# RMSNorm, memory-bound: all loads and stores on one hardware queue, in a fixed order, with rows of up to 64 KB

## The chip, the cores and the metric

One core of one Trainium2 chip. The metric is the device time of one execution in microseconds (us). The kernel before takes 165.03 us (median of 4 runs, 164.47 to 165.42). Times of one kernel scatter by about 1 us here, so most kernels were timed in five rounds beside the kernel before.

## The reference

```python
batch, seq, dim = 16, 1024, 512            # 16384 rows of 512 float32
rms = np.sqrt(np.mean(x ** 2, axis=-1, keepdims=True) + 1e-5)
return (x / rms * gamma).astype(np.float32)
```

33.55 MB are read and 33.55 MB written. Nothing is reused, so the transfers alone set a floor.

## The kernel before

Eight tiles of 16 rows per partition (4 MB) go through five buffers. Four engines matter here: SyncE, which only issues transfers, ACT (ScalarE), DVE (VectorE) and POOL (GpSimd). SyncE issues the loads on its hardware queue. POOL issues the stores, 2 MB each, on the software queue. (A queue is also called a ring below.) ACT squares and sums each row, and takes the root of 8 sums at a time. DVE takes the reciprocal and multiplies by it and by gamma, in place.

```python
work = ctx.enter_context(tc.tile_pool(name="work", bufs=5))
...                                                    # cut: pools, gamma broadcast over partitions
nc.gpsimd.dma_start(out=gamma_row, in_=gamma.unsqueeze(0))
...
for t in range(ntiles):                                # 8 tiles
    xt = work.tile([P, G, R, D], fp32)                 # G=2, R=8, D=512
    nc.sync.dma_start(out=xt, in_=xt_view[t].rearrange("p (g r) d -> p g r d", g=G))
    ...
    for g in range(G):
        for r in range(R):
            nc.scalar.activation(out=sq_scratch, in_=xt[:, g, r, :], func=AF.Square,
                                 accum_out=ss[:, g, r : r + 1])
        nc.scalar.activation(out=rms[:, g], in_=ss[:, g], func=AF.Sqrt, bias=eps_t, scale=1.0 / D)
        nc.vector.reciprocal(out=rstd[:, g], in_=rms[:, g])
        for r in range(R):
            nc.vector.scalar_tensor_tensor(out=xt[:, g, r, :], in0=xt[:, g, r, :],
                scalar=rstd[:, g, r : r + 1], in1=gamma_b, op0=OP.mult, op1=OP.mult)
        nc.gpsimd.dma_start(out=ot_view[t][:, g], in_=xt[:, g])
```

## Time and profile before

| | before |
|---|---|
| time, median | 165.03 us |
| span of the profiled run | 163.2 us |
| DVE, ACT busy | 90.4 us, 98.5 us |
| DMA, mean over the span | 411 GB/s |

The first view is the page's table of 40 slices of the span, with its list of DMA queues. A digit is the busy share of the 16 DMA engines in a slice, in tenths; a queue's line gives packets, MB and share of the engines' time.

```profile
span 163.2 us, 536 instructions
...
DMA  7999899999999999999999999999999999999980
GB/s 241 402 442 458 385 474 426 317 440 426 466 414 415 426 446 458 418 409 474 383 418 454 462 426 393 478 389 413 422 434 430 426 442 430 426 434 434 430 369 28
...
q1 hardware_dynamic: 1152, 33.55, 48.6%
q0 software_dynamic: 2336, 33.56, 48.2%
q14 instruction: 3, 0.02, 0.0%
```

The engines are busy in all but the first and the last slices: the kernel is bound by transfers. Two queues share them half and half. The last queue line: three packets of 8 KB on a queue that the program does not use, which the list calls instruction: fetches of instructions. In the packet records they stand at 34.8, 51.8 and 79.4 us, 0.31 us each.

The second view gives busy times in stretches of the span; the last two columns are the mean share of the DMA engines and the rate (PEclk, the clock of TensorE, plays no part here). (A packet seems to be booked whole at its start, so shares over 1 occur.)

```profile
core 0: us, PE busy (x) PEld busy (x) DVE busy (x) ACT busy (x) POOL busy (x), PEclk, DMA share, GB/s
40.00:60.00 20.00, 0.00 (x0) 0.00 (x0) 18.11 (x30) 19.21 (x55) 1.59 (x3) 1.00 1.00 430
60.00:80.00 20.00, 0.00 (x0) 0.00 (x0) 18.10 (x30) 16.12 (x48) 1.59 (x3) 1.00 1.00 429
80.00:100.00 20.00, 0.00 (x0) 0.00 (x0) 13.50 (x22) 11.89 (x34) 1.59 (x3) 1.00 1.01 434
...
158.00:160.00 2.00, 0.00 (x0) 0.00 (x0) 0.00 (x0) 0.00 (x0) 0.00 (x0) 1.00 0.39 164
160.00:162.00 2.00, 0.00 (x0) 0.00 (x0) 0.00 (x0) 0.00 (x0) 0.00 (x0) 1.00 0.06 25
```

In the middle the rate is 429 to 434 GB/s, with loads and stores mixed. The stretch 158 to 160 us has a share of only 0.39, but 160 to 162 us still 0.06: a few engines work on after the others have finished. The records of semaphores show this by engine. Each bulk transfer has 16 such records, read here as one for each engine, when its share of the transfer had landed; these are the 16 times of the last store, sorted (us from the span's start; worked out from the trace, not a view of the page):

```
before: 158.87 158.93 158.96 159.04 159.05 159.06 159.13 159.16 159.17 159.18 159.33 159.34 159.36 160.62 161.41 161.73
```

Thirteen engines end within 0.5 us. Three are 1.3 to 2.4 us later than the last of these. The transfer is done when the last is. From here on, "spread" is the distance from the first to the last of these 16 times; the prediction calls it skew.

The waits of SyncE's queue show when loads had to wait for a free buffer (total us, times, longest):

```profile
SPq L59 <- DMA out_dram<-xt: 97.6, 3, 58.0
```

Three of the eight loads waited for stores to land. The engines had stores to move meanwhile, so this cost nothing by itself.

### The profile page before, as it was taken

The numbers are of one execution on the slowest core, as the hardware profiler recorded it, in microseconds if no ns is written. First come the engines' busy times: TensorE is split into PE (matmuls) and PEld (weight loads), VectorE is DVE, ScalarE is ACT, GpSimd is POOL, SyncE is SP. The second block draws the span as 40 slices with busy tenths as digits, with TensorE's granted clock in tenths as the row PEclk, the third lists the DMA queues.
The fourth block names the chain that finished last, engine by engine and source line by source line (L and its number), as shares of the span: only waits on it lengthen the run. The fifth ranks groups of instructions, "written<-read, shape, count | busy, mean of one in ns | idle before, by whom it ended". The sixth has DMA issues, their size and how long they took to land.

```text
span 163.2 us, 536 instructions
## 1 busy us (share of the span) xinstructions
PE 2.0 (1%) x2; PEld 0.5 (0%) x2; DVE 90.4 (55%) x147; ACT 98.5 (60%) x274; POOL 9.3 (6%) x21
## 2 busy tenths in 40 slices
PE   0050000000000000000000000000000000000000
PEld 0010000000000000000000000000000000000000
DVE  0010098988988988988918890058930298600000
ACT  3007999999999999997499601998008992000000
POOL 2000001011011011011010101001010001100000
DMA  7999899999999999999999999999999999999980
GB/s 241 402 442 458 385 474 426 317 440 426 466 414 415 426 446 458 418 409 474 383 418 454 462 426 393 478 389 413 422 434 430 426 442 430 426 434 434 430 369 28
DMA packets 3491, 67.14 MB, mean 411 GB/s; under 512 B 416, under 2 KB 416, under 8 KB 416
## 3 DMA queue, kind: packets, MB, share of 16 engines
q1 hardware_dynamic: 1152, 33.55, 48.6%
q0 software_dynamic: 2336, 33.56, 48.2%
q14 instruction: 3, 0.02, 0.0%
HBM read 33.56 MB, written 33.55 MB: 411 GB/s over the span
## 4 chain that ended last, share of the span: by engine, by line
DMA 47%; ACT 19%; issue 16%; DVE 3%; POOL 1%; POOLq 0%; SPq 0%
DMA out_dram<-xt 27%; DMA xt<-in_x_dram 21%; ACT sq_scratch L67 17%; DVE xt L84 3%; ACT rms L74 1%; ACT L74 1%; POOL out_dram L93 1%; POOLq L119 0%; DVE rstd L81 0%; POOLq L93 0%; SPq L59 0%
## 5 line engine op out<-in xcount | busy, mean ns | idle before, releaser
L67 ACT ACTIVATE sq_scratch<-xt 128x512 f32<-128x512 f32 x128 | 80.4, 628 | 35.8 <-DMA xt<-in_x_dram 32.3
L84 DVE SCALAR_TENSOR_TENSOR xt<-xt,rstd,gamma_b 128x512 f32<-128x512 f32 x128 | 86.2, 747 | 0.6
L81 DVE RECIPROCAL rstd<-rms 128x8 f32<-128x8 f32 x16 | 3.2, 203 | 40.2 <-ACT rms L74 40.2
L67 ACT ACTIVATION_READ_ACCUMULATOR sq_scratch<-xt 128x1 f32 x128 | 23.9, 186 | 0.0
L93 POOL DMA_DIRECT2D out_dram<-xt x16 | 8.5, 532 | 131.7 <-DVE xt L84 131.7
L51 DVE COPY gamma_b<-gamma_psum 128x512 f32<-128x512 f32 x1 | 0.7, 693 | 9.4 <-PE gamma_psum L49 9.4
L74 ACT ACTIVATE rms<-ss,eps_t 128x8 f32<-128x8 f32 x16 | 4.8, 301 | 0.5
L49 PE MATMUL gamma_psum<-gamma_row,ones_col 1*128 1x512 f32 x2 | 2.0, 1122 | 8.3 <-DMA gamma_row<-in_gamma_dram 8.3
L67 ACT ACT_TABLE_LOAD x1 | 1.3, 1283 | 0.7 <-PEq L108 0.7
L74 ACT ACT_TABLE_LOAD x1 | 1.3, 1283 | 0.0
L45 POOL DMA_DIRECT2D gamma_row<-in_gamma_dram x1 | 0.6, 616 | 0.8 <-POOLq L108 0.8
L47 DVE MEMSET ones_col<- 1x128 f32 x1 | 0.2, 165 | 0.8 <-PEq L108 0.8
L49 PEld LDWEIGHTS gamma_psum<-gamma_row,ones_col 1*128 1x128 f32 x2 | 0.5, 306 | 8.2 <-issue 8.2
L108 POOL MEMSET const-float32-0.0<- 128x1 f32 x1 | 0.1, 98 | 0.2 <-issue 0.2
L108 POOL MEMSET const-bfloat16-1.0<- 128x1 bf16 x1 | 0.1, 101 | 0.0
L108 POOL MEMSET const-float32-1.0<- 128x1 f32 x1 | 0.1, 98 | 0.0
L108 POOL MEMSET const-uint8-127<- 128x1 uint8 x1 | 0.1, 98 | 0.0
L54 DVE MEMSET eps_t<- 128x1 f32 x1 | 0.1, 59 | 0.0
## 6 DMA issues: line engine op xcount, KB each, us to landing
xt<-in_x_dram SPq DMA_DIRECT2D x8, 4096.0 KB, 21.4
out_dram<-xt POOLq DMA_DIRECT2D x16, 2048.0 KB, 37.5
gamma_row<-in_gamma_dram POOLq DMA_DIRECT2D x1, 2.0 KB, 6.9
```

The lines of the kernel that those rows point to most:

```text
L45: nc.gpsimd.dma_start(out=gamma_row, in_=gamma.unsqueeze(0))
L47: nc.vector.memset(ones_col, 1.0)
L49: nc.tensor.matmul(gamma_psum, ones_col, gamma_row, start=True, stop=True)
L51: nc.vector.tensor_copy(out=gamma_b, in_=gamma_psum)
L54: nc.vector.memset(eps_t, eps)
L67: nc.scalar.activation(out=sq_scratch, in_=xt[:, g, r, :], func=AF.Square, accum_out=ss[:, g, r : r + 1],)
L74: nc.scalar.activation(out=rms[:, g], in_=ss[:, g], func=AF.Sqrt, bias=eps_t, scale=1.0 / D,)
L81: nc.vector.reciprocal(out=rstd[:, g], in_=rms[:, g])
L84: nc.vector.scalar_tensor_tensor(out=xt[:, g, r, :], in0=xt[:, g, r, :], scalar=rstd[:, g, r : r + 1], in1=gamma_b, op0=OP.mult, op1=OP.mult,)
L93: nc.gpsimd.dma_start(out=ot_view[t][:, g], in_=xt[:, g])
L108: nc = _bacc.Bacc("TRN2", target_bir_lowering=False, num_devices=1)
```

## The change

The intent is to keep the DMA engines busy without a break and in a planned order. Every load and store goes on SyncE's one hardware queue. Three slots of 32 rows per partition (8 MB) hold the data, so 24 MB are loaded ahead. A row of a transfer is 64 KB or 32 KB per partition, where it was 32 KB for loads and 16 KB for stores. Gamma moves to ACT's queue. The instructions of ACT and DVE stay the same in number and size.

```diff
-    work = ctx.enter_context(tc.tile_pool(name="work", bufs=5))
+    slots = [const.tile([P, R, D], fp32, name=f"slot{i}") for i in range(3)]   # R = 32
+    def load(t, slot, r0, r1):
+        nc.sync.dma_start(out=slots[slot][:, r0:r1], in_=xv[t][:, r0:r1])
+    def store(t, slot, r0, r1):
+        nc.sync.dma_start(out=ov[t][:, r0:r1], in_=slots[slot][:, r0:r1])
+    load(0, 0, 0, 16)
+    load(0, 0, 16, 32)
+    load(1, 1, 0, 32)
+    load(2, 2, 0, 32)
...                                          # cut: views of x and out
-    nc.gpsimd.dma_start(out=gamma_row, in_=gamma.unsqueeze(0))
+    nc.scalar.dma_start(out=gamma_row, in_=gamma.unsqueeze(0))
...                                          # cut: compute(), the same instructions on 8 rows at a time
-            nc.gpsimd.dma_start(out=ot_view[t][:, g], in_=xt[:, g])
+    compute(0, 0, 32)
+    store(0, 0, 0, 32)
+    compute(1, 0, 16)
+    store(1, 1, 0, 16)
+    load(3, 0, 0, 16)
+    load(3, 0, 16, 32)
+    compute(1, 16, 32)
+    store(1, 1, 16, 32)
+    compute(2, 0, 32)
+    store(2, 2, 0, 32)
+    compute(0, 0, 16)
+    store(3, 0, 0, 16)
+    compute(0, 16, 32)
+    store(3, 0, 16, 32)
```

More of the change, by code (lines that the diff above doesn't have):

```diff
@@ L27 @@
     N, D = xf.shape
-    assert N % P == 0
-    R = 8
-    G = 2
-    RG = R * G
-    assert N % (P * RG) == 0
-    ntiles = N // (P * RG)
-    xt_view = xf.rearrange("(t p r) d -> t p r d", p=P, r=RG)
-    ot_view = of.rearrange("(t p g r) d -> t p g r d", p=P, g=G, r=R)
+    R = 32
+    G = 8
+    assert N == 4 * P * R
+    xv = xf.rearrange("(t p r) d -> t p r d", p=P, r=R)
+    ov = of.rearrange("(t p r) d -> t p r d", p=P, r=R)
     const = ctx.enter_context(tc.tile_pool(name="const", bufs=1))
-    work = ctx.enter_context(tc.tile_pool(name="work", bufs=5))
     stats = ctx.enter_context(tc.tile_pool(name="stats", bufs=4))
     psum = ctx.enter_context(tc.tile_pool(name="psum", bufs=1, space=bass.MemoryType.PSUM))
+    slots = [const.tile([P, R, D], fp32, name=f"slot{i}") for i in range(3)]
[7 more added lines that the diff above has]
+    load(2, 2, 0, 32)
     gamma_row = const.tile([1, D], fp32)
-    nc.gpsimd.dma_start(out=gamma_row, in_=gamma.unsqueeze(0))
+    nc.scalar.dma_start(out=gamma_row, in_=gamma.unsqueeze(0))
     ones_col = const.tile([1, P], fp32)
@@ L55, with compute @@
     sq_scratch = const.tile([P, D], fp32)
-    for t in range(ntiles):
-        xt = work.tile([P, G, R, D], fp32)
-        nc.sync.dma_start(out=xt, in_=xt_view[t].rearrange("p (g r) d -> p g r d", g=G))
-        ss = stats.tile([P, G, R], fp32)
-        rms = stats.tile([P, G, R], fp32)
-        rstd = stats.tile([P, G, R], fp32)
-        for g in range(G):
-            for r in range(R):
+    def compute(slot, r0, r1):
+        for g in range(r0, r1, G):
+            ss = stats.tile([P, G], fp32, name="ss")
+            rms = stats.tile([P, G], fp32, name="rms")
+            rstd = stats.tile([P, G], fp32, name="rstd")
+            for r in range(G):
                 nc.scalar.activation(
                     out=sq_scratch,
-                    in_=xt[:, g, r, :],
+                    in_=slots[slot][:, g + r, :],
                     func=AF.Square,
-                    accum_out=ss[:, g, r : r + 1],
+                    accum_out=ss[:, r : r + 1],
                 )
-            nc.scalar.activation(
-                out=rms[:, g],
-                in_=ss[:, g],
-                func=AF.Sqrt,
-                bias=eps_t,
-                scale=1.0 / D,
-            )
-            nc.vector.reciprocal(out=rstd[:, g], in_=rms[:, g])
-            for r in range(R):
+            nc.scalar.activation(out=rms, in_=ss, func=AF.Sqrt, bias=eps_t, scale=1.0 / D)
+            nc.vector.reciprocal(out=rstd, in_=rms)
+            for r in range(G):
                 nc.vector.scalar_tensor_tensor(
-                    out=xt[:, g, r, :],
-                    in0=xt[:, g, r, :],
-                    scalar=rstd[:, g, r : r + 1],
+                    out=slots[slot][:, g + r, :],
+                    in0=slots[slot][:, g + r, :],
+                    scalar=rstd[:, r : r + 1],
                     in1=gamma_b,
```

## The prediction

> **What bounds it.** The 16 DMA engines. The slice table of the page shows DMA at 9 tenths or more in all but four of 40; 67.1 MB move in the 163.2 us span. ACT is busy 98.5 us and DVE 90.4 us (page, part 1) and fit under the transfers. The trace's completions give the rate of one direction alone: the 4-MB loads landed at 12.99 and 22.71 us, 9.72 us apart (432 GB/s), and in the tail, where only stores remain, a 2-MB store lands each 4.86 us (432 GB/s). The stretches 40-60, 60-80 and 80-100 us, with loads and stores mixed, ran at 430, 429 and 434 GB/s. The Trainium skill ("DMA: Bandwidth & Descriptors", section "Where 436 GB/s comes from") puts the ceiling at 435.2 GB/s, within 1% of this trace.
>
> **Budget of before.** 67.1 MB at 432 GB/s: 155.3 us. First packet at 1.73 us. Last landing 161.73 us, then 1.5 us to the span's end. That leaves 4.7 us: first packets 0.6 us longer than the usual 1.21; about 0.7 us of slow load packets at 29-31 us, when the first stores start; about 0.35 us from last packet to landing; some 0.6 us more in the mixed part; and 2.4 us of skew: from the load landing at 123 us on, 13 of the 16 engines complete each transfer within 0.6 us, the other three 1.2 to 2.4 us later.
>
> **What the change does.**
> - Stores leave the software queue: 16 POOL issues of 0.53 us go. They were hidden; SyncE issues of 0.4 us are too: nothing.
> - Packets of 64 KB: a 32-KB packet takes 1.213 us, a 16-KB one 0.611, so at most 9 ns per packet to save; 90 fewer per engine would be 0.8 us, but the landing cadence shows none of it.
> - One queue in a fixed order: engines stop alternating between two rings. The mixed losses become two or three changes of direction. The skew may go if it comes from two rings or from the software queue (the same page, "Latency and other measured facts", calls two engines usually slower, and that specific to the software path; this trace has three late ones, cause not shown). The 8-KB instruction fetches (0.31 us, three in the run) stay.
> - No wait runs the queue dry (estimates from 9.7 us per 4 MB, 6.2 us per 8 rows): loads queued to 60 us, store 0 ready at 45; store 0 ends at 79, next store ready at 60; loads of the fourth block issue at about 80.5 (after store 0 landed), needed at 89; later stores ready at 73, 98, 119, 131, needed at 108, 118, 137, 147. Smallest slack 8 us.
>
> **On the critical path.** Only the 4.7 us residue. I expect 1.2 to 3.5 us of it back. The time (165.19) is 1.9 us over the span; I keep that.
>
> **Predicted** 162.5 us, range 160.6 to 164.4; faster by over 2% 0.33, within 2% 0.65, slower 0.02.
>
> **Right or wrong in the profile.** DMA at 9 tenths in all middle slices; last store's 16 completions within 0.8 us (else the skew is not the queue's); the last landing at 157.5 to 159.5 us; 64-KB packets of 2.41 to 2.43 us; SyncE's longest wait about 45 us before store 0.
>
> **What would make it wrong.** 64-KB rows (256 KB between engines' streams) could run at another HBM rate, either way; changes of direction could drain the engines for over 1 us each; the skew could stay.

## The result

163.16 us (median of 4 runs, 162.68 to 163.86) against 165.03 us. The ratio is 0.9887, with a 95% interval of 0.9852 to 0.9921: a real gain of about 1.1%, within 2%. A ratio here is the mean time of one kernel's runs over that of the other's of the same rounds, so not quite the ratio of the medians quoted. Executions over 1.5% slower than the fastest of the same kernel are left out of the means. A second run of five rounds gave 163.32 us and 0.9904.

The same views after. The page's slices and queues:

```profile
span 161.6 us, 509 instructions
...
DMA  7999999989989999699699999999999799699991
GB/s 260 389 430 478 389 470 438 519 375 405 519 373 405 505 276 487 292 519 487 292 440 454 389 454 454 389 478 430 389 503 519 308 487 503 292 462 430 405 470 49
...
q1 hardware_dynamic: 1728, 67.11, 97.3%
q14 instruction: 3, 0.02, 0.0%
```

One queue now carries all data, in 1728 packets where two queues had 3488. The three instruction fetches are still there. Slices at 6 and 7 tenths in the middle are not idle engines: with 64-KB packets booked at their start a slice can miss or gain a whole packet. The rates over longer stretches show that:

```profile
40.00:60.00 20.00, 0.00 (x0) 0.00 (x0) 15.46 (x26) 16.99 (x48) 0.00 (x0) 1.00 1.04 420
60.00:80.00 20.00, 0.00 (x0) 0.00 (x0) 17.48 (x29) 19.18 (x56) 0.00 (x0) 1.00 0.97 419
80.00:100.00 20.00, 0.00 (x0) 0.00 (x0) 16.62 (x27) 11.77 (x34) 0.00 (x0) 1.00 0.97 417
...
158.00:160.00 2.00, 0.00 (x0) 0.00 (x0) 0.00 (x0) 0.00 (x0) 0.00 (x0) 1.00 0.08 33
160.00:162.00 2.00, 0.00 (x0) 0.00 (x0) 0.00 (x0) 0.00 (x0) 0.00 (x0) 1.00 0.00 0
```

The middle has not become faster: 417 to 420 GB/s here against 429 to 434 before, within what the booking of whole packets can shift (one 64-KB packet on each of 16 engines is 1 MB, or 52 GB/s over 20 us). In the tail 160 to 162 us is empty, where it held 0.06. (The last packets are 32 KB in place of 16, so they are booked earlier, and the share of 158 to 160 us can't be compared with before.) The firm reading is by engine, the last store's 16 landings in the profiled run:

```
after: 158.64 158.68 158.78 158.85 158.86 158.91 158.99 159.01 159.09 159.10 159.13 159.18 159.40 159.54 160.26 160.63
```

The median engine ends as before (159.05 against 159.17 us). Two engines are late in place of three, and by less. The waits of SyncE's queue:

```profile
SPq L44 <- DVE slot L79: 81.7, 5, 22.3
...
SPq L44 <- DMA slot<-in_x_dram: 23.6, 2, 19.9
SPq L41 <- DMA out_dram<-slot: 21.7, 1, 21.7
```

SyncE waits for loads and then for DVE before each store (lines 44 are stores, 41 loads), and once 21.7 us for store 0 to land before it may reload slot 0. None of these leaves the queue dry: the fourth block's loads were issued at 82.6 us, and the store ahead of them in the queue landed at 91 to 92 us.

### The profile page after: what moved, and what is told of

The parts are those of the page before. It is cut to its first block, busy times and chain, and to the rows that moved or that the text cites. A ratio compares the mean times of both kernels' runs of the same rounds, so it can differ in the third digit from the quotient of the medians.

```text
span 161.6 us, 509 instructions
## 1 busy us (share of the span) xinstructions
PE 2.0 (1%) x2; PEld 0.5 (0%) x2; DVE 90.4 (56%) x147; ACT 98.5 (61%) x274; POOL 0.2 (0%) x4
## 3 DMA queue, kind: packets, MB, share of 16 engines
q1 hardware_dynamic: 1728, 67.11, 97.3%
## 4 chain that ended last, share of the span: by engine, by line
DMA 43%; ACT 20%; DVE 17%; issue 2%; DVEq 0%
DMA out_dram<-slot 23%; DMA slot<-in_x_dram 19%; ACT sq_scratch L70 18%; DVE slot L79 16%; ACT rms L76 2%; ACT L76 1%; DVE rstd L77 1%; DVEq L127 0%
## 5 line engine op out<-in xcount | busy, mean ns | idle before, releaser
L70 ACT ACTIVATE sq_scratch<-slot 128x512 f32<-128x512 f32 x128 | 80.5, 629 | 26.8 <-DMA slot<-in_x_dram 23.2
L79 DVE SCALAR_TENSOR_TENSOR slot<-slot,rstd,gamma_b 128x512 f32<-128x512 f32 x128 | 86.2, 747 | 0.6
L70 ACT ACTIVATION_READ_ACCUMULATOR sq_scratch<-slot 128x1 f32 x128 | 23.9, 187 | 0.0
```

The costliest lines, as they stand in the source:

```text
L70: nc.scalar.activation(out=sq_scratch, in_=slots[slot][:, g + r, :], func=AF.Square, accum_out=ss[:, r : r + 1],)
L79: nc.vector.scalar_tensor_tensor(out=slots[slot][:, g + r, :], in0=slots[slot][:, g + r, :], scalar=rstd[:, r : r + 1], in1=gamma_b, op0=O ...
```

## The experiments

The theory from the prediction was that some of the lost time comes from two rings that alternate or from the software queue, and goes away with one hardware queue. Rivals: the packets are larger; or something else makes engines late. Twelve runs were made, in three jobs; the kernel before had a median of 164.97, 165.00 and 164.85 us in them, so times of different jobs can be compared to about 0.15 us. Medians are of all runs of a kernel.

| kernel | median us | ratio to before | 95% interval |
|---|---|---|---|
| changed kernel again | 163.32 | 0.9904 | 0.9878 to 0.9930 |
| stores on POOL | 163.22 | 0.9901 | 0.9874 to 0.9929 |
| rows of 32 KB | 163.73 | 0.9919 | 0.9893 to 0.9945 |
| early small store | 163.73 | 0.9930 | 0.9906 to 0.9954 |
| gamma on POOL | 163.91 | 0.9939 | 0.9916 to 0.9963 |
| products of 8 rows at once | 163.22 | 0.9900 | 0.9875 to 0.9925 |
| two hardware queues, mended | 172.32 | 1.0442 | 1.0417 to 1.0468 |
| copy only (wrong result) | 162.15 | 0.9824 | 0.9803 to 0.9846 |
| copy, stores on POOL (wrong result) | 162.70 | 0.9846 | 0.9816 to 0.9876 |
| same instructions on 8 columns (wrong result) | 163.54 | 0.9921 | 0.9891 to 0.9951 |

Not in the table are the kernel before once more (one run, 164.80 us, state unknown) and the two hardware queues before they were mended (190.06 us, ratio 1.1527). One of the five runs of the mended kernel was a slow one (176.74 us), and two of the six of the copy with its stores on POOL.

### The two kernels once more

The changed kernel was timed again beside the next three:

> The changed kernel itself, timed in the rounds of the next three, so that they can be compared with it. All theories: ratio to before 0.985 to 0.992; last landing about 160.6 us; the last store's 16 completions spread over 1 to 2 us.

The time came as expected; the last landing and the spread did not. The landing was at 161.29 us, 0.7 us later than in the first trace, and the spread was 2.6 us. The kernel before, run once for a second trace:

> The kernel before once more, for a second trace. If its three late engines (1.2 to 2.4 us behind the other 13 at the end) belong to the kernel, they are there again, 2 us or more between the first and the last completion of the last store, and the span ends 1.5 us after the last landing. If they are chance, the spread differs by over 1 us from the first trace's 2.9 us.

164.80 us. Again three late engines, by 1.5 to 2.2 us behind the median, spread 2.5 us. So the late engines were not chance of one run. The span again ended 1.5 us after the last landing. With two traces of each kernel the gain can be split:

| us | before, two traces | after, two traces | gain of the means |
|---|---|---|---|
| median engine's last landing | 159.17, 159.35 | 159.05, 159.01 | 0.23 |
| last engine, behind the median | 2.56, 2.16 | 1.58, 2.28 | 0.43 |
| end of span, behind the last landing | 1.52, 1.51 | 1.01, 1.01 | 0.51 |
| span | 163.25, 163.02 | 161.64, 162.30 | 1.17 |

Over all timed runs of that job the mean span fell from 163.17 (11 runs) to 161.70 us (6 runs), by 1.47 us. The traces thus place about 1.2 us of the 1.5; the late engines differ from run to run, and two traces are few.

### Stores on POOL

```diff
     def store(t, slot, r0, r1):
-        nc.sync.dma_start(out=ov[t][:, r0:r1], in_=slots[slot][:, r0:r1])
+        nc.gpsimd.dma_start(out=ov[t][:, r0:r1], in_=slots[slot][:, r0:r1])
```

> The changed kernel with its stores issued by POOL (software queue) again, in the same order and shape. Theory 1 (what was gained came from the stores leaving the software queue: less skew between the 16 engines, and a shorter end): the skew of the last store goes back to about 2.4 us and the span's end to 1.5 us after the last landing, time within 0.4 us of before. Theory 2 (the gain came from the layout, the 64-KB packets and the fixed order): the time stays within 0.5 us of the changed kernel.

163.22 us, in the same rounds as the changed kernel's 163.32. Theory 1 falls as a statement about the time: leaving the software queue is not what the time needs. But the trace shows two effects that cancel. POOL's issues (start us, us, engine, line, and the idle time before with its releaser), the last two:

```profile
125.10 0.53 POOL L44 DMA_DIRECT2D out_dram<-slot  x1 [16.86 <-DVE slot L79]
149.28 0.53 POOL L44 DMA_DIRECT2D out_dram<-slot  x1 [23.65 <-DVE slot L79]
```

The last store was issued only at 149.28 us, when the store before it had already landed on most engines (148.9 to 150.1 us). The cause is the order: with two rings a load shares the engines with stores, so the last load landed at 127 to 131 us, where it landed at 110 to 112 us in the changed kernel; ACT and DVE came late with the last 16 rows. In the gap that this left the late engines caught up, and all 16 landed the last store within 0.17 us. The span ended 1.3 us after the last landing, 1.0 us with all on SyncE.

### Two hardware queues

```diff
-        nc.sync.dma_start(out=slots[slot][:, r0:r1], in_=xv[t][:, r0:r1])
+        nc.scalar.dma_start(out=slots[slot][:, r0:r1], in_=xv[t][:, r0:r1])
...
-    load(3, 0, 0, 16)
-    load(3, 0, 16, 32)
...
-    compute(2, 0, 32)
+    compute(2, 0, 16)
+    load(3, 0, 0, 16)
+    load(3, 0, 16, 32)
+    compute(2, 16, 32)
```

> The changed kernel with its loads on ACT's hardware queue and its stores on SyncE's, so two rings alternate but neither is the software queue. If alternating between two rings makes the skew and the mixed losses: skew over 2 us, the time 0.7 us or more over the changed kernel. If only the software queue does: skew and time within 0.4 us of the changed kernel. Rival of both (skew is from instruction fetches): skew unchanged here and in the run with POOL stores, 1 to 2 us in both.

190.06 us, by a mistake of the experiment. The lines of its page for the DMA engines and for the matmul that needs gamma:

```profile
DMA  6999999999995000005999999989999989979994
...
L56 PE MATMUL gamma_psum<-gamma_row,ones_col 1*128 1x512 f32 x2 | 2.0, 1121 | 61.1 <-DMA gamma_row<-in_gamma_dram 61.1
```

Gamma was still issued from ACT, now behind 24 MB of loads in the same ring, and arrived at about 61 us: in this run the ring was served in order, and 2 KB waited for 24 MB. DVE could not start, and the engines ran dry. The run says nothing on the question it was made for. Mended, with gamma first on SyncE's queue:

```diff
-    nc.scalar.dma_start(out=gamma_row, in_=gamma.unsqueeze(0))
+    nc.sync.dma_start(out=gamma_row, in_=gamma.unsqueeze(0))
```

> The run with two hardware rings mended: gamma goes ahead of the stores on SyncE's queue, no longer behind 24 MB of loads. The run with POOL stores equalled the changed kernel, so the software queue costs nothing in the middle; then two hardware rings should equal it too: within 0.6 us of the changed kernel, a last spread of 0.5 to 2 us, and an end 1.0 us after the last landing as in the changed kernel (1.3 us with POOL stores, 1.5 before). If two rings on hardware cost by alternating, over 0.8 us slower.

172.32 us, a miss of 9 us. The stretches of the profile near the end, columns as before (third and fourth busy times are DVE and ACT; the last two are DMA share and rate), and the longest waits of DVE:

```profile
140.00:150.00 10.00, 0.00 (x0) 0.00 (x0) 3.72 (x7) 9.59 (x28) 0.00 (x0) 1.00 0.88 380
150.00:158.00 8.00, 0.00 (x0) 0.00 (x0) 7.36 (x12) 2.35 (x7) 0.00 (x0) 1.00 0.02 8
158.00:170.00 12.00, 0.00 (x0) 0.00 (x0) 0.10 (x1) 0.00 (x0) 0.00 (x0) 1.00 0.82 350
```

```profile
DVE rstd L77 <- ACT rms L76: 62.7, 16, 17.3
```

From 150 to 158 us the engines move hardly anything: DVE works on the last rows. ACT issued the fourth block's loads at 86.5 and 87.3 us, and they then alternated with stores; the last one landed at 136.5 to 139.9 us, where the changed kernel had 110 to 112. So most of the loss is the order again, not a slower rate. (The edit also moved these loads, which ACT issues 4 us later than SyncE did at 82.6 us.) It does not settle whether two rings alternate at a cost of their own.

### Packet size

```diff
-    xv = xf.rearrange("(t p r) d -> t p r d", p=P, r=R)                       # out likewise
+    xv = xf.rearrange("(t h p r) d -> t h p r d", p=P, h=2, r=R // 2)
-        nc.sync.dma_start(out=slots[slot][:, r0:r1], in_=xv[t][:, r0:r1])     # store likewise
+        for h in range(r0 // 16, r1 // 16):
+            nc.sync.dma_start(out=slots[slot][:, 16 * h : 16 * h + 16], in_=xv[t][h])
```

> The changed kernel with rows of 32 KB per partition in 4-MB transfers, same order on the same queue. If the 64-KB packets gave part of the gain, 9 ns per packet would cost 16 of the 64-KB packets per load half and store half, about 0.3 us in all; I expect the time within 0.4 us of the changed kernel: packet size gives nothing.

163.73 us, 0.4 us above the changed kernel's 163.32 of another job, and the intervals of the two ratios overlap. Packets of 32 KB took 1.213 us, of 64 KB 2.418 us. The size gives nothing that these runs can resolve.

### Where loads and stores first meet

In the changed kernel's packet records, 16 load packets that start at 57.9 to 59.0 us, one on each engine, take 3.3 to 4.0 us in place of 2.42: 1.3 us lost on each engine on average just before the first store packets. The kernel before has the like at 29 to 33 us, 0.8 us per engine. The next change from loads to stores, at 109 us, costs hardly anything: five slow packets, 0.2 to 0.35 us each.

```diff
+    first = const.tile([P, P], fp32)
+    nc.vector.memset(first, 0.0)
+    nc.scalar.dma_start(out=ov[3][:, R - 1, :P], in_=first)
     gamma_row = const.tile([1, D], fp32)
```

> The changed kernel with a 64-KB store issued from ACT at the very start, to rows that a later store overwrites. In the changed kernel the last load packets before the first store take 3.7 us in place of 2.42, 1.3 us on each engine; the second change from loads to stores at 110 us costs almost nothing. Theory A (the first writes of a run are slow, whatever comes before): the early store takes this cost, hidden or cheaper, the slow packets at 58 to 62 us are gone and the time falls by 0.7 to 1.3 us. Theory B (a long row of loads followed by stores costs this at that place): slow packets and time stay, within 0.3 us.

163.73 us, and the slow packets at 58 to 63 us are all there. Theory A falls, at least for a store of 64 KB. The time is 0.4 us above the changed kernel's in the same rounds, a little over theory B's 0.3, with overlapping intervals. Theory B as stated does not cover the other runs: with stores on POOL the slow packets came at 47 to 52 us, when the first bulk store met loads of the other ring; and in the unmended run with two hardware queues the first stores met idle engines at 87 us and only one packet was slow, by 0.33 us; 16 slow packets came at 111 us, as the loads came back beside them. So in every trace most of the loss comes once, when loads and stores first meet in bulk: 1.1 to 1.4 us per engine in most, 0.7 with rows of 32 KB, 0.8 to 0.9 in the kernel before, in the unmended run and on 8 columns (below). The two runs with two hardware queues lose another 0.5 us per engine at 117 to 133 us. What it is stays open.

### Copy only: what remains without compute

The calls of `compute` were emptied, so x is copied to out. The loads, stores and their order stay. Its output is wrong, which doesn't matter for the time.

```diff
     def compute(slot, r0, r1):
-        for g in range(r0, r1, G):
-            ...                                  # cut: all of it
+        pass
```

> Wrong result on purpose: the changed kernel without squares, roots and products, so x is copied to out by the same loads and stores in the same order on the one queue. It has too few instructions to fetch more while it runs. If the late engines of the changed kernel come from the 8-KB instruction fetches (0.31 us each at 34, 53 and 83 us in its trace), no fetch is in the trace, the last store's 16 completions lie within 0.7 us (2.0 to 2.6 us in the changed kernel), and the time is 0.8 to 1.8 us below it. If they come from the queue or the engines themselves, the spread stays over 1.2 us and the time within 0.5 us. Either way the slow load packets at 58 to 62 us stay.

162.15 us, four runs within 0.2 us. The page's span and queues, and the tail in the stretches:

```profile
span 160.2 us, 67 instructions
...
q1 hardware_dynamic: 1728, 67.11, 98.1%
q10 hardware_dynamic: 2, 0.00, 0.0%
```

```profile
158.00:160.00 2.00, 0.00 (x0) 0.00 (x0) 0.00 (x0) 0.00 (x0) 1.00 0.00 0
160.00:162.00 2.00, 0.00 (x0) 0.00 (x0) 0.00 (x0) 0.00 (x0) 1.00 0.00 0
```

There is no instruction queue in the list, and no engine starts a data packet after 158 us. The last store's landings:

```
copy: 158.67 158.81 158.82 158.86 158.87 158.88 158.96 158.99 159.02 159.05 159.07 159.16 159.17 159.18 159.21 159.22
```

The spread is 0.55 us. The median engine is where it was. So the late engines and the 1.2 us (163.32 - 162.15) go together with the compute instructions, and not with the queue. The slow load packets at 58 to 62 us stayed, as expected.

### The same instructions on 8 columns

The copy took away both the instruction fetches and ACT's and DVE's use of the memory. This kernel puts the instructions back and leaves the use of memory out.

```diff
-                    out=sq_scratch, in_=slots[slot][:, g + r, :],
+                    out=sq_scratch[:, :8], in_=slots[slot][:, g + r, :8],
...
-                    out=slots[slot][:, g + r, :], in0=slots[slot][:, g + r, :], ... in1=gamma_b,
+                    out=slots[slot][:, g + r, :8], in0=slots[slot][:, g + r, :8], ... in1=gamma_b[:, :8],
```

> Wrong result on purpose: the changed kernel with every instruction kept, but squares and products on 8 of the 512 columns of each row, so ACT and DVE hardly touch the buffers while the instructions are fetched as before. If the 1.2 us that the copy gained come from the missing instruction fetches: three 8-KB fetches in the trace, one to three late engines, 1.0 to 2.5 us between first and last completion of the last store, time within 0.5 us of the changed kernel (163.3). If they come from ACT and DVE working on the same memory: spread under 0.7 us and the time about 162.2, as in the copy.

163.54 us: the time of the changed kernel is back, though ACT and DVE touch one part in 64 of the data. Its page:

```profile
span 161.0 us, 509 instructions
...
q14 instruction: 3, 0.02, 0.0%
```

The three fetches are back, at 29.1, 51.1 and 73.8 us, and so are two late engines: 14 landings of the last store at 158.42 to 159.08 us, then 159.39 and 159.94. In the packet records a single 64-KB packet at 51.4 us is 0.53 us too long; it starts as the second fetch ends, and the next landing of loads has one engine 0.8 us behind the others (63.04 against 61.67 to 62.21 us). So the instruction stream, not the traffic of compute, is what makes engines late.

The traces show that it is the fetch itself. In all 12 traces with fetches, each of the 36 is followed at once by a data packet that takes 0.11 to 0.66 us too long. And although a packet's record does not name its engine, a packet of a busy engine starts 3 to 4 ns before the recorded end of the one before it. By this the packets can be strung into 16 chains of 4 MB each, one for each engine. In the second trace of the changed kernel, where no link on the two late chains is ambiguous, it gives (worked out from the trace, not a view of the page; us):

```
chain         fetches at      next packet too long by   last packet ends
late 1        34.00, 82.94    0.31, 0.12                160.01
late 2        53.56           0.63                      160.97
the other 14  none                                      158.33 to 158.98
```

The chains that hold the fetches are the late ones, and their delays add up. The first lost 0.31 + 0.31 us with its first fetch, 0.31 + 0.12 with its second, and 0.39 at 110 us, less 0.1 where stores begin: 1.34 us, measured 1.33 behind the median. The second lost 0.31 + 0.63 us with its fetch, 0.47 more than the others where stores begin, and 0.75 at 109 us: 2.16 us, measured 2.29. The first trace, the early small store and this kernel on 8 columns give the same two chains. With rows of 32 KB only one of three engines with a fetch stayed late (by 2.2 us); with gamma on POOL (below) too many links are ambiguous to tell. The first trace of the kernel before differs: of its three late chains two hold the fetches, but the one that is 2.3 us late holds none and lost 1.8 us at 104 to 108 us, soon after the last load was issued at 102 us. A few links there are ambiguous. So that two rings made one engine late in the kernel before stays possible.

### Copy with the stores on POOL

Two rings alternate here for most of the run, without fetches.

> Wrong result on purpose: the copy with its stores issued by POOL, so loads and stores alternate between two rings with no instruction fetch in the run. If late engines need a fetch to start: last spread under 0.8 us, and the time within 0.5 us of the copy on one queue (162.15). If the alternation of two rings makes late engines or losses by itself: spread over 1.2 us or the time over 0.8 us above the copy.

The profiled run has a spread of 0.53 us and a span of 160.4 us, like the copy on one queue, and no slow packets but the first of the run and those where loads and stores first meet:

```profile
span 160.4 us, 71 instructions
...
q1 hardware_dynamic: 864, 33.55, 49.5%
q0 software_dynamic: 864, 33.55, 48.4%
q10 hardware_dynamic: 2, 0.00, 0.0%
```

So two rings, one of them the software queue, do not by themselves make engines late, in this trace. The four fast runs are 162.01, 162.12, 162.26 and 163.13 us, a median of 162.19, like the copy's 162.15. The two slow ones, 164.52 and 164.58 us, are left out; why they are slow is open, as the profiled run was a fast one.

### Gamma on POOL

```diff
-    nc.scalar.dma_start(out=gamma_row, in_=gamma.unsqueeze(0))
+    nc.gpsimd.dma_start(out=gamma_row, in_=gamma.unsqueeze(0))
```

> The changed kernel with gamma, 2 KB, loaded from POOL as in the kernel before, the only use of the software queue. If the 0.5 us by which the changed kernel ends sooner after its last landing (1.0 us, before 1.5 us) belong to POOL's use of the software queue at all, the distance is 1.3 to 1.5 us here; if to having stores on it, 1.0 us. Time within 0.6 us of the changed kernel either way.

163.91 us, 0.6 us above the changed kernel's 163.32 of another job, with overlapping intervals; the end came 1.13 us after the last landing, between both expectations and nearer to the second. Over the traces the distance is 0.9 to 1.0 us with no transfer on the software queue (eight kernels, both two-queue runs among them), 1.1 with gamma alone, 1.2 to 1.3 with six stores, 1.5 with gamma and sixteen stores. It grows with the transfers on the software queue; why was not tested.

### Fewer instructions, correct result

```diff
+            if whole:                              # slots 1 and 2
+                xg = slots[slot][:, g : g + G, :]
+                nc.vector.tensor_tensor(out=xg, in0=xg, in1=rstd.unsqueeze(2).to_broadcast([P, G, D]), op=OP.mult)
+                nc.vector.tensor_tensor(out=xg, in0=xg, in1=gamma_b.unsqueeze(1).to_broadcast([P, G, D]), op=OP.mult)
+                continue
             for r in range(G):
                 nc.vector.scalar_tensor_tensor(
```

> A correct kernel that needs fewer instructions: the changed kernel with the products of the second and third slot as two DVE instructions per 8 rows, in place of 8. DVE falls from 147 to 99 instructions and rises to about 110 to 125 us busy, estimated from 747 ns per 512 columns; its results stay ahead of the queue by 1 us or more. If late engines come from fetches, at least one of the three fetches is gone from the trace, and the time is 0.2 to 0.6 us below the changed kernel; if all three stay, the time is the same within 0.3 us. If DVE gets too slow, stores wait and the time rises by over 1 us.

163.22 us against 163.32 for the changed kernel of another job: the same. A miss: DVE has 48 instructions fewer, but the page still lists three fetches:

```profile
q14 instruction: 3, 0.02, 0.0%
...
L81 DVE TENSOR_TENSOR slot<-slot,gamma_b 128x4096 f32<-128x4096 f32 x8 | 35.4, 4425 | 0.1
L80 DVE TENSOR_TENSOR slot<-slot,rstd 128x4096 f32<-128x4096 f32 x8 | 35.4, 4421 | 0.1
```

One fetch moved from 53 to 85 us; none went. One engine was 1.3 us late at the end (161.19 against 159.76 to 159.93 us); strung into chains as above, it is the one that carried two of the fetches. The other 15 ended 0.8 us later than in the changed kernel, as the store of slot 2 came late from the slower DVE: on these engines it landed at 140.3 to 140.5 us, where the changed kernel had 139.3 to 140.2 on its 14 punctual ones. The two products of 8 rows take 4.42 us each (35.4 us in 8), 8.85 us in all, against 8 x 0.748 = 5.98 us.

No correct kernel here beats the changed one beyond its noise. The copy's 162.15 us shows how little is left: 1.2 us.

## Why the prediction was right, and where it was not

The time held: 162.5 us predicted, 163.16 measured, within 160.6 to 164.4 and within 2% of before. The range is 3.8 us wide and the gain was under 2 us, so that the time lies in it says little for the mechanism; that it came within 0.7 us of the estimate is in part luck, as two misses of opposite sign show below. Point by point:

- **The bound.** "The 16 DMA engines." Right. The copy, with no compute at all, is only 1.8% faster than the kernel before.
- **Only the residue can come back.** "Only the 4.7 us residue. I expect 1.2 to 3.5 us of it back." Right as a frame: 1.65 to 1.87 us came (differences of the medians). The middle of that range was too high, by the next points.
- **The skew.** "last store's 16 completions within 0.8 us (else the skew is not the queue's)". This step failed, and the clause in brackets is the answer: the spread was 2.0 and 2.6 us. "The skew may go if it comes from two rings or from the software queue" is what the experiments refuted for the changed kernel: the copy has a spread of 0.53 to 0.55 us with one queue or with two rings, and the instruction stream brings the late engines back, on the engines that carried the fetches. (For one of the three late engines of the kernel before, two rings stay possible.) The prediction knew the fetches and counted 0.31 us each. The instruction stream cost 1.2 us of time, four times one fetch. The chains show how 0.31 us becomes 1.3 to 2.3 us on an engine: the packet after each fetch is too long as well, one engine carries two fetches, and late engines have more slow packets where loads and stores change. Why these packets are slow is not shown.
- **Changes of direction.** "The mixed losses become two or three changes of direction." Mis-sized: the first meeting of loads and stores cost 1.3 us per engine, where it had cost 0.8 to 0.9 before (0.7 in the prediction's budget); the later ones cost about 0.1.
- **The last landing.** "at 157.5 to 159.5 us". Measured 160.6 and 161.3; the sum of the two points above. The median engine, at 159.0, lies inside.
- **The end.** "then 1.5 us to the span's end" was carried over as a constant. It fell to 1.0 us, a gain that the prediction did not have, the largest of the three parts in the table (0.51 of 1.17 us), and which by luck brought the total back towards the estimate while the last landing was 1.1 to 1.8 us past its range.
- **Packets.** "64-KB packets of 2.41 to 2.43 us": 2.418, the median. No gain from size: rows of 32 KB cost nothing measurable.
- **No dry queue.** Right. "SyncE's longest wait about 45 us before store 0" comes as two lines of the waits, 19.9 us for the load and 22.3 us for DVE, until 44.85 us. The loads of the fourth block were issued at 82.6 us, predicted 80.5, with 8 to 9 us to spare.
- **"DMA at 9 tenths in all middle slices"** failed in the letter, as shown: 64-KB packets make the slices uneven.

The Trainium skill's page "DMA: Bandwidth & Descriptors", section "Where 436 GB/s comes from", gives a ceiling of 435.2 GB/s for the 16 ports of the on-chip memory. Just below it: 9.7 us per 4 MB, 432 GB/s, for loads, stores, both queues and all three packet sizes. An estimate from these rates: a kernel that already averages 411 GB/s over its span can gain 5% at most (432 to 411), and only in its head, its tail, its late engines and where loads and stores meet.

## What to carry to other kernels

When a kernel runs at the rate of the DMA engines, read the tail engine by engine before planning a change of queues: the time is set by the latest engine, and in the changed kernel what made it late was the fetching of instructions, not the data's queue. A single queue in a fixed order did not move bytes faster, but it kept stores from delaying the last loads; with loads and stores on two rings that order was lost, and the end starved for up to 8 us. An improvement of 1% needs a control of the same kind as the copy here, which says how much is there to be had at all.

## What the Trainium skill lacked or had wrong

- "Runtime: NRT & Kernel Launch", section "Instruction fetch mechanics", calls the cost of fetching more instructions "mostly hidden" and says blocks of 16 KiB. The fetches are single packets of 8192 bytes, about 0.31 us each, three in a run, on the data's DMA engines, and the data packet after each of them takes 0.11 to 0.66 us too long. The copy, which has no fetches and no compute, is 1.2 us faster (162.15 against 163.32 us), and the instructions on 8 columns bring the time back (163.54 us). For a kernel bound by DMA the page should say that they are not free.
- "DMA: Bandwidth & Descriptors", section "Latency and other measured facts", puts slow engines down to the software queue, as a best guess. Here two engines are 1 to 2 us late with all data on a hardware queue (spread 2.0 and 2.6 us), and they are those that ran the instruction fetches; none are late in the profiled copy with its stores on the software queue (0.53 us). The records name no engines, so whether the page's two engines are among them is not shown.
- The same page, section "Issuing engines are not separate DMA queues", says that several issuing engines save only issue time. No section of the page gives a figure for what they can cost through the order: loads and stores on two hardware rings took 172.32 us where one ring took 163.32 us, as stores delayed the last loads, and gamma behind 24 MB in one ring arrived at 61 us.
- No page that I read tells of the loss where loads and stores first meet in bulk: 0.7 to 1.4 us on each engine, mainly once in a run, in all traces. Its cause is open.
- No page that I read tells that the end of the program comes later when the software queue was used: 0.9 to 1.0 us after the last landing without it, 1.5 us with 17 transfers on it.
